# A gated feed-forward half in seven block products: the first pair's weights come through ACT's queue, and the tiles of a pair change places

## The chip, the core and the metric

The kernel runs on one core of a Trainium2 chip. Its engines are TensorE (PE in the profile, PEld for its weight loads), VectorE (DVE), ScalarE (ACT), GpSimd (POOL) and SyncE (SP). SP, ACT and POOL can each issue transfers between the chip's main memory and the core's on-chip memory; an engine's instructions, transfers among them, are taken in program order. The metric is the time of one execution on the device in microseconds (us).

## The reference

One decoder layer for 512 tokens of width 1024. Its first and last parts are feed-forward halves with a gate, and between them lie a gated linear recurrence with a short convolution, and attention into 256 memory rows. The change touches the two feed-forward halves alone:

```python
def swiglu(h, w_gate, w_up, w_down):
    return (jax.nn.silu(h @ w_gate) * (h @ w_up)) @ w_down
...
x = x + 0.5 * swiglu(rms_norm(x, ffn1_norm[l]), ffn1_gate[l], ffn1_up[l], ffn1_down[l])
...
x = x + 0.5 * swiglu(rms_norm(x, ffn2_norm[l]), ffn2_gate[l], ffn2_up[l], ffn2_down[l])
```

The hidden width is 2816, which is 22 tiles of 128.

## The kernel before, in words

Every float32 operand is split into a rounded high part and a low part that holds the rest (names that end in `h` and `l`, or `whi` and `wlo`), and a product is the sum of three: high by high, high weight by low input, low weight by high input. ACT makes the high part with a copy, DVE the low part with a subtraction that reads ACT's result. So no matmul of a weight tile starts before ACT's copy, and none with its `wlo` before DVE's subtraction.

The class `Half` holds a feed-forward half. Its hidden tiles 0 to 3 are computed plainly (`product`, `finish`). The other 18 go in 9 pairs, m = 4, 6, ..., 20 (`seven`). In a pair, gate and up weights and the input are cut into blocks, and seven block products take the place of eight: p1, p5, r6, p2, r7, p4, p3. Each is 24 matmuls with 256 columns. They need five weight tiles of 512 KB in all: b11, b22 and b21 are blocks as they lie in memory. t1 is a sum of two blocks: a plain transfer brings the first, and a second transfer, issued by POOL, adds the other to it as it lands. t3 is made in the same way, both transfers by POOL. p1 multiplies b11 by input `a11`, p5 multiplies t1 by `q1`, r6 multiplies t1 + b22 (DVE adds) by `n2`, p2 multiplies b21 by `a12`, r7 multiplies t3 by `d3`, p4 takes t1 + b22 + b21 by `a22`, and p3 takes b22 by `q4`.

`load` (line 293) issues the transfers of a pair. `unit` (line 312) splits a weight tile: the copy on ACT is line 316, the subtraction on DVE line 317. Matmuls of all seven products are line 338, the sum t1 + b22 is an addition from line 324.

Ahead of the first pair, `inputs_steps` (line 246) combines the normed input into the blocks that the products take. For that it uses six raw tiles: `xa0`, `qn0`, `xa1`, `qn1`, and the combinations `c0`, `c1`. They have the same tag as the weight tiles, in a ring of six (tag `raw`, line 257 and line 297), so the five weight tiles of pair 4 can only be loaded as these are given back. `quad` (line 236) splits an input block, ACT at line 242 and DVE at line 243. Blocks `a11`, `q1`, `n2` are split early; the splits of the other four are the list `later` (lines 285 to 289). `a12` and `a22` read `tx`, which is not in this ring; `d3` and `q4` read `c0` and `c1`, which are.

All this is done beside `down_pairs` (line 433): while PE multiplies the first four hidden tiles by the down weights in four steps (d = 0, 2, 4, 6; names `psd`, lines 119 to 121), three of the waiting steps are issued after each d. After d = 6 stands p1 of pair 4.

The text of the program is not the order in which an engine gets its instructions: a scheduler lays them out when the program is built, each engine's list is then fixed, and between engines only the waits order them. The places that matter below are those lists.

Of the kernel before, what the change touches and what calls it, by code (L numbers as in the profile page):

```python
# [38 lines left out]
def decoder_layer(ctx: ExitStack, tc: tile.TileContext, xT, memT, vecs, masks, ident_d,  # L39
                  w1, w1d, w_in, w_i, w_out, w_q, w_k, w_v, w_o, w2, w2d, gfin, out):  # L40
    nc = tc.nc
# [44 lines left out]
    def weights(src, shape):  # L86

        raw, hi, lo, load, split = weight_steps(src, shape)
        load(0, shape[0])
        split(0, shape[0])  # L90
        return hi, lo

    def weight_steps(src, shape):
        n = n_unit[0]
        n_unit[0] += 1
        raw = wpool.tile([P, 1024], F32, tag="raw", name=f"raw{n}")
        hi, lo = (wpool.tile([P, 1024], F32R, tag=t, name=f"{t}{n}") for t in ("whi", "wlo"))
        a, b = shape
        w = a * b

        def load(k0, k1, queue=nc.sync):
            c = slice(k0 * b, k1 * b)
            if len(src.shape) == 3:
                queue.dma_start(raw[:, c].rearrange("p (a b) -> p a b", a=src.shape[1]), src)
            else:
                queue.dma_start(raw[:, c], src[:, c])

        def split(k0, k1):
            c = slice(k0 * b, k1 * b)
            nc.scalar.activation(hi[:, c], raw[:, c], AF.Copy)  # L110
            nc.vector.tensor_tensor(lo[:, c], raw[:, c], r32(hi[:, c]), ALU.subtract)  # L111

        v = lambda t: t[:, :w].rearrange("p (a b) -> p a b", b=b)
        return raw, v(hi), v(lo), load, split
# [80 lines left out]
    CLASSIC = 4  # L195
    PARTS = ((0, 4), (4, 10), (10, 16), (16, FT))

    class Half:
# [47 lines left out]
        def inputs_steps(self):  # L246

            name, hp = self.name, self.hp
            self.q, later = {}, []
            sub = lambda o, a, b: nc.vector.tensor_tensor(o, a, b, ALU.subtract)  # L250

            def scaled(t, k):
                nc.vector.scalar_tensor_tensor(t, x[k], vec[:, self.gcol + k:self.gcol + k + 1], self.bc,
                                               op0=ALU.mult, op1=ALU.mult)


            raw = lambda key: hp.tile([P, 2, S], F32, tag="raw", name=f"{key}_{name}", bufs=6)
            self.tx = [hp.tile([P, 2, S], F32, tag=t, name=f"x{t}_{name}", bufs=4) for t in ("ah", "al")]
            tmps = [(raw(f"xa{n}"), raw(f"qn{n}")) for n in range(2)]
            self.tc = [raw(f"c{n}") for n in range(2)]  # L260
            steps = []
            for n in range(2):
                xb, comb = self.tx[n], self.tc[n]
                xa, qn = tmps[n]
                q1, n2 = qn[:, :, :256], qn[:, :, 256:]

                def one(n=n, xa=xa):
                    for i in range(2):
                        scaled(xa[:, i], 2 * n + i)
                    self.quad("a11", n, xa[:, :, :256])  # L270

                def two(n=n, xb=xb, xa=xa, q1=q1, n2=n2):
                    for i in range(2):
                        scaled(xb[:, i], 4 + 2 * n + i)
                    sub(q1, xa[:, :, 256:], xb[:, :, 256:])
                    sub(n2, q1, xa[:, :, :256])
                    self.quad("q1", n, q1)

                def three(n=n, xb=xb, comb=comb, xa=xa, n2=n2):
                    sub(comb[:, :, :256], xa[:, :, :256], xa[:, :, 256:])  # L280
                    nc.vector.tensor_tensor(comb[:, :, 256:], xb[:, :, :256], n2, ALU.add)
                    self.quad("n2", n, n2)

                steps += [one, two, three]
            for key in ("a12", "d3", "a22", "q4"):
                for n in range(2):
                    t = (self.tx if key[0] == "a" else self.tc)[n]
                    h = t[:, :, :256] if key in ("a12", "d3") else t[:, :, 256:]
                    later.append(lambda key=key, n=n, h=h: self.quad(key, n, h))
            return steps, later  # L290


        def load(self, m):


            def tile(key):
                return self.hp.tile([P, 2, 512], F32, tag="raw", name=f"{key}_{self.name}{m}", bufs=6)

            def src(j, h):
                return self.wgu[m:m + 2, j, :, h * 512:(h + 1) * 512].rearrange("m p c -> p m c")  # L300

            b11, t1, b22, b21, t3 = (tile(k) for k in ("b11", "t1", "b22", "b21", "t3"))
            nc.sync.dma_start(b11, src(0, 0))
            nc.sync.dma_start(t1, src(0, 0))
            nc.gpsimd.dma_start(t1, src(1, 0), accum_op=ALU.add)
            nc.sync.dma_start(b22, src(1, 1))
            nc.sync.dma_start(b21, src(0, 1))
            nc.gpsimd.dma_start(t3, src(1, 0))
            nc.gpsimd.dma_start(t3, src(1, 1), accum_op=ALU.add)
            return dict(b11=b11, t1=t1, b22=b22, b21=b21, t3=t3)  # L310

        def unit(self, raw):
# [250 lines left out]
    with tc.tile_pool(name="mix", bufs=8, reuse_waits="tile") as mp:  # L563
# [56 lines left out]
        for k2 in range(KT // 2):  # L620
            wh, wl = weights(w_i[k2], (2, 512))
            for kk in range(2):
                k = 2 * k2 + kk
# [512 lines left out]
```

## Time and profile before

| | |
|---|---|
| median of 3 runs | 1113.97 us (1113.47 to 1115.74) |
| the profiled execution, its own time | 1115.02 us |
| span of the profiled execution | 1113.2 us |
| PE busy | 1094.7 us |
| DVE busy | 731.2 us |
| ACT busy | 485.9 us |
| POOL busy | 74.6 us |
| mean granted clock of PE | 0.995 |

The span is the time from the first to the last instruction. A row of the timeline gives start, duration, engine, source line, operation, the tile written and the tiles read, and in brackets how long the engine stood idle before it and what ended that. PE's matmuls overlap: a matmul of 256 columns is shown with 0.28 us, yet the next one starts 0.12 us after it, so the distance between starts counts. "Landing" is the time from the issue of a transfer to its completion as the waiting engine sees it.

### The profile page before, as it was taken

What the parts mean: (1) busy time and instruction counts of PE and PEld (TensorE: products, weight loads), DVE (VectorE), ACT (ScalarE), POOL (GpSimd) and SP (SyncE); (2) the same over time, 40 slices, a digit from 0 to 9 for tenths busy, and PEclk for the clock granted to TensorE, in tenths of its full rate; (3) what the DMA queues carried; (4) which work ended last, traced back from release to release, by engine and by line L of the source; (5) the groups of instructions that cost most, each with busy time, mean ns of one, the idle gap of its engine ahead of it and who ended that gap; (6) DMA issues with size and microseconds to landing.
All of it is one profiled execution on the core that took longest, in us unless ns stands there. A gap on an engine that the chain in (4) does not pass through costs nothing. (4 is left out here: it accounts for less than half of the span.)

```text
span 1113.2 us, 15967 instructions
## 1 busy us (share of the span) xinstructions
PE 1094.7 (98%) x6528; PEld 979.4 (88%) x6528; DVE 731.2 (66%) x980; ACT 485.9 (44%) x667; POOL 74.6 (7%) x75
## 2 busy tenths in 40 slices
PE   9989999999999999999999999999989999999997
PEld 7869998998998888888889888888889989989995
DVE  6786755764768566885686556554987747755744
ACT  6435533542545344323364345342545524533553
POOL 0001100110100000000100000000011101100102
PEclk9999999999999999999999999999999999999999
DMA  6467764673523332222244324232287835764521
GB/s 210 127 177 172 195 143 125 164 194 116 160 45 110 97 100 80 81 76 85 67 120 138 122 77 133 74 96 78 84 230 190 186 109 137 203 146 135 114 76 76
DMA packets 68745, 140.53 MB, mean 126 GB/s; under 512 B 4944, under 2 KB 20560, under 8 KB 68672
## 3 DMA queue, kind: packets, MB, share of 16 engines
q1 hardware_dynamic: 54112, 108.02, 30.7%
q0 software_dynamic: 12544, 28.84, 13.2%
q10 hardware_dynamic: 2016, 2.66, 0.7%
q8 instruction: 51, 0.84, 0.3%
q14 instruction: 22, 0.18, 0.1%
HBM read 137.40 MB, written 2.10 MB: 125 GB/s over the span
## 5 line engine op out<-in xcount | busy, mean ns | idle before, releaser
L110 ACT ACTIVATE whi<-raw 128x1024 fp32r<-128x1024 f32 (+4 forms) x143 | 138.0, 970 | 329.5 <-issue 67.4
L111 DVE TENSOR_TENSOR wlo<-raw,whi 128x1024 fp32r<-128x1024 f32 (+4 forms) x143 | 158.6, 1112 | 83.7 <-ACT whi L110 83.1
L316 ACT ACTIVATE whi<-b_f 128x1024 fp32r<-128x1024 f32 x72 | 76.3, 1060 | 104.5 <-issue 34.3
L317 DVE TENSOR_TENSOR wlo<-b_f,whi 128x1024 fp32r<-128x1024 f32 x72 | 88.2, 1225 | 42.3 <-ACT whi L316 40.9
L120 PE MATMUL psd_f<-al_f,whi 128*128 128x512 f32 x280 | 109.1, 390 | 0.0
L121 PE MATMUL psd_f<-ah_f,wlo 128*128 128x512 f32 x280 | 109.1, 390 | 0.0
L119 PE MATMUL psd_f<-ah_f,whi 128*128 128x512 f32 x280 | 108.5, 390 | 0.0
L317 DVE TENSOR_TENSOR wlo<-t_f,whi 128x1024 fp32r<-128x1024 f32 x54 | 66.1, 1224 | 42.6 <-ACT whi L316 42.6
L192 DVE SCALAR_TENSOR_TENSOR xall<-psd_f,xall 128x512 f32<-128x512 f32 x52 | 35.4, 691 | 71.4 <-PE psd_f L121 71.4
L316 ACT ACTIVATE whi<-t_f 128x1024 fp32r<-128x1024 f32 x54 | 57.0, 1056 | 56.6 <-issue 21.3
L121 PEld LDWEIGHTS psd_f<-ah_f,wlo 128*128 128x128 f32 x280 | 52.6, 188 | 10.9
L119 PEld LDWEIGHTS psd_f<-ah_f,whi 128*128 128x128 f32 x280 | 52.6, 188 | 10.8
L120 PEld LDWEIGHTS psd_f<-al_f,whi 128*128 128x128 f32 x280 | 52.6, 188 | 10.7
L338 PE MATMUL psD_f<-q1h_f,whi 128*128 128x256 f32 x144 | 41.2, 286 | 8.3 <-ACT whi L316 8.3
L338 PE MATMUL psA_f<-a11h_f,wlo 128*128 128x256 f32 x144 | 42.2, 293 | 0.0
L338 PE MATMUL psA_f<-a11h_f,whi 128*128 128x256 f32 x144 | 42.1, 292 | 0.0
L338 PE MATMUL psA_f<-a11l_f,whi 128*128 128x256 f32 x144 | 42.1, 292 | 0.0
L338 PE MATMUL psD_f<-q1l_f,whi 128*128 128x256 f32 x144 | 41.0, 284 | 0.0
L338 PE MATMUL psA_f<-a22h_f,whi 128*128 128x256 f32 x144 | 40.9, 284 | 0.0
L338 PE MATMUL psD_f<-q4h_f,wlo 128*128 128x256 f32 x144 | 40.8, 284 | 0.0
L338 PE MATMUL psA_f<-n2h_f,wlo 128*128 128x256 f32 x144 | 40.8, 284 | 0.0
L338 PE MATMUL psA_f<-a22h_f,wlo 128*128 128x256 f32 x144 | 40.8, 284 | 0.0
(778 smaller groups left out, 3209.7 us busy)
## 6 DMA issues: line engine op xcount, KB each, us to landing
b_f<-in_w SPq DMA_DIRECT2D x54, 512.0 KB, 4.0
t_f<-in_w POOLq DMA_DIRECT2D x54, 512.0 KB, 5.7
raw<-in_w_in SPq DMA_DIRECT2D x24, 512.0 KB, 3.5
t_f<-in_w SPq DMA_DIRECT2D x18, 512.0 KB, 5.3
raw<-in_w1d SPq DMA_DIRECT2D x20, 384.0 KB, 3.1
raw<-in_w SPq DMA_DIRECT2D x13, 512.0 KB, 3.5
raw<-in_w2d SPq DMA_DIRECT2D x16, 384.0 KB, 3.1
raw<-in_w2d SPq DMA_DIRECT2D x10, 512.0 KB, 3.4
```

Of the source, the lines that this page charges most:

```text
L110: nc.scalar.activation(hi[:, c], raw[:, c], AF.Copy)
L111: nc.vector.tensor_tensor(lo[:, c], raw[:, c], r32(hi[:, c]), ALU.subtract)
L119: nc.tensor.matmul(out, lhsT=wh, rhs=xh, start=first, stop=False)
L120: nc.tensor.matmul(out, lhsT=wh, rhs=xl, start=False, stop=False)
L121: nc.tensor.matmul(out, lhsT=wl, rhs=xh, start=False, stop=last)
L192: nc.vector.scalar_tensor_tensor(x[k], ps, scale, x[k], op0=ALU.mult, op1=ALU.add)
L316: nc.scalar.activation(hi, raw, AF.Copy)
L317: nc.vector.tensor_tensor(lo, raw, r32(hi), ALU.subtract)
L338: nc.tensor.matmul(o, lhsT=a[:, i, w], rhs=b, start=first and i == 0 and k == 0 and n == 0, stop=k == 3 and n == 2, skip_group_check=True)
```

## The change

Three things are changed, all in `Half`:

- the splits of the input blocks in `later` come in another order: `d3` and `q4` of c0, then of c1, then `a12` and `a22`;
- in every pair, t3 takes its tile from the ring ahead of b22 and b21, and its two transfers are written ahead of those of b22 and b21;
- for pair 4 alone (`CLASSIC` is 4), the transfers of b11, t1 and b22 are issued by ACT. b21 stays with SP, and the other pairs stay with SP as they were.

```diff
-            for key in ("a12", "d3", "a22", "q4"):
-                for n in range(2):
+            for keys in (("d3", "q4"), ("a12", "a22")):
+                for n, key in ((n, key) for n in range(2) for key in keys):
                     t = (self.tx if key[0] == "a" else self.tc)[n]
                     h = t[:, :, :256] if key in ("a12", "d3") else t[:, :, 256:]
                     later.append(lambda key=key, n=n, h=h: self.quad(key, n, h))
...
-            b11, t1, b22, b21, t3 = (tile(k) for k in ("b11", "t1", "b22", "b21", "t3"))
-            nc.sync.dma_start(b11, src(0, 0))
-            nc.sync.dma_start(t1, src(0, 0))
+            b11, t1, t3, b22, b21 = (tile(k) for k in ("b11", "t1", "t3", "b22", "b21"))
+
+            queue = nc.scalar if m == CLASSIC else nc.sync
+            queue.dma_start(b11, src(0, 0))
+            queue.dma_start(t1, src(0, 0))
             nc.gpsimd.dma_start(t1, src(1, 0), accum_op=ALU.add)
-            nc.sync.dma_start(b22, src(1, 1))
-            nc.sync.dma_start(b21, src(0, 1))
             nc.gpsimd.dma_start(t3, src(1, 0))
             nc.gpsimd.dma_start(t3, src(1, 1), accum_op=ALU.add)
+            queue.dma_start(b22, src(1, 1))
+            nc.sync.dma_start(b21, src(0, 1))
```

Lines behind the change have numbers higher by two (before's lines 316 and 338 are 318 and 340). The lists of the engines move as follows; the first half's pair 4 is shown, and the second half's moves alike. In the names, `f1` is the first half, the digit behind it the pair or the block half, and the last number a running one.

ACT's list ahead of pair 4, before. The five rows with a `c` or `x` tile behind the arrow are input splits, the last two the copies of b11 and t1; no transfer stands here, since SP issues all four plain ones.

```order
L242 ACTIVATE n2h_f11_624<-qn1_f1_407 128x512
L242 ACTIVATE d3h_f11_668<-c1_f1_409 128x512
L242 ACTIVATE a22h_f10_672<-xah_f1_402 128x512
L242 ACTIVATE a22h_f11_704<-xal_f1_403 128x512
L242 ACTIVATE q4h_f10_708<-c0_f1_408 128x512
L242 ACTIVATE q4h_f11_712<-c1_f1_409 128x512
L316 ACTIVATE whi12_729<-b11_f14_716 128x1024
L316 ACTIVATE whi13_760<-t1_f14_717 128x1024
```

The same place of the change:

```order
L242 ACTIVATE n2h_f11_624<-qn1_f1_407 128x512
L305 DMA b11_f14_716<-in_w1 128x2x512
L242 ACTIVATE d3h_f11_664<-c1_f1_409 128x512
L242 ACTIVATE q4h_f11_668<-c1_f1_409 128x512
L242 ACTIVATE a12h_f10_672<-xah_f1_402 128x512
L242 ACTIVATE a22h_f10_704<-xah_f1_402 128x512
L242 ACTIVATE a12h_f11_708<-xal_f1_403 128x512
L242 ACTIVATE a22h_f11_712<-xal_f1_403 128x512
L306 DMA t1_f14_717<-in_w1 128x2x512
L310 DMA b22_f14_719<-in_w1 128x2x512
L318 ACTIVATE whi12_729<-b11_f14_716 128x1024
L318 ACTIVATE whi13_760<-t1_f14_717 128x1024
```

The transfer of b11 stands behind the last split of `n2`; that of t1 stands behind six further splits, of which the first two read `c1`. On POOL, t3's plain transfer now stands ahead of the adding transfer of t1; on SP, b21 of pair 4 stands alone ahead of pair 6.

PE's list at the start of p1, before: `a11` with b11's halves (whi12, wlo12) is p1, `q1` with t1's (whi13, wlo13) is p5.

```order
L338 MATMUL psA_f14_728<-a11h_f10_430,whi12_729 128x256
L338 MATMUL psA_f14_728<-a11l_f10_431,whi12_729 128x256
L338 MATMUL psD_f14_759<-q1h_f10_510,whi13_760 128x256
L338 MATMUL psD_f14_759<-q1l_f10_511,whi13_760 128x256
L338 MATMUL psA_f14_728<-a11h_f10_430,wlo12_730 128x256
```

And of the change:

```order
L340 MATMUL psA_f14_728<-a11h_f10_430,whi12_729 128x256
L340 MATMUL psA_f14_728<-a11l_f10_431,whi12_729 128x256
L340 MATMUL psA_f14_728<-a11h_f10_430,wlo12_730 128x256
L340 MATMUL psA_f14_728<-a11h_f10_430,whi12_729 128x256
L340 MATMUL psA_f14_728<-a11l_f10_431,whi12_729 128x256
```

The two `q1` matmuls that stood third and fourth are now behind all 24 of `a11`. Instead, two matmuls of p2 (b21, `a12`) stand after the first two of r6 (t1 + b22, `n2`):

```order
L340 MATMUL psA_f14_728<-n2l_f10_571,whi14_789 128x256
L340 MATMUL psB_f14_819<-a12h_f10_672,whi15_820 128x256
L340 MATMUL psB_f14_819<-a12l_f10_673,whi15_820 128x256
L340 MATMUL psA_f14_728<-n2h_f10_570,wlo14_790 128x256
```

DVE's list keeps its length up to b11's `wlo`: the same number of splits and additions stands ahead of it, the splits in the new order.

At the program's start, ACT's list has a transfer behind splits and squares, the same in both programs:

```order
L125 ACTIVATE x_f14h_202<-xall_102,vec_97 128x512
L125 ACTIVATE x_f15h_215<-xall_102,vec_97 128x512
L125 ACTIVATE x_f16h_228<-xall_102,vec_97 128x512
L125 ACTIVATE x_f17h_241<-xall_102,vec_97 128x512
L136 ACTIVATE sq_f1_254<-xall_102 128x512
L136 ACTIVATE sq_f1_258<-xall_102 128x512
L502 DMA ident_99<-in_ident_d 128x128
```

Five activations stand between `x_f14h` and the transfer of `ident`; the change leaves this place as it is.

## The prediction

> **What bounds the kernel now.** I read the page's list of engines first, then the waits of PE, then the timeline of each engine around the two places that the waits name. The page:
>
> ```profile
> span 1113.2 us, 15967 instructions
> PE 1094.7 (98%) x6528; PEld 979.4 (88%) x6528; DVE 731.2 (66%) x980; ACT 485.9 (44%) x667; POOL 74.6 (7%) x75
> ```
>
> PE stands idle for 18.5 us in all. The waits of PE, the whole list (who waited, for whom, us in total, times, longest):
>
> ```profile
> PE psD_f L338 <- ACT whi L316: 8.3, 2, 5.0
> PE ps_f L119 <- ACT whi L110: 1.6, 2, 0.8
> PE warm L71 <- DVE mhalf L61: 1.1, 1, 1.1
> PE psw L119 <- ACT yh1h L811: 0.5, 1, 0.5
> ```
>
> Only the first row lies in the pairs of block products, twice: once in each half, in pair 4. The other 16 pairs have no wait on PE. So all that the change can gain lies at two places, and what it costs elsewhere must first use up slack. The first place, by PE's rows (MATMUL alone):
>
> ```profile
> 75.95 0.28 PE L338 MATMUL psA_f<-a11h_f,whi 128*128 128x256 f32 x1
> ...
> 76.07 0.28 PE L338 MATMUL psA_f<-a11l_f,whi 128*128 128x256 f32 x1
> 81.37 0.53 PE L338 MATMUL psD_f<-q1h_f,whi 128*128 128x256 f32 x1 [5.02 <-ACT whi L316]
> ...
> 82.77 0.41 PE L338 MATMUL psA_f<-a11h_f,whi 128*128 128x256 f32 x1
> 82.98 0.42 PE L338 MATMUL psA_f<-a11l_f,whi 128*128 128x256 f32 x1
> ...
> 94.24 0.28 PE L338 MATMUL psA_f<-d3h_f,whi 128*128 128x256 f32 x1
> ```
>
> After two matmuls of `a11` PE is held by the first of `q1`, which needs t1, and 22 matmuls of `a11` that need only b11 stand behind it. Then matmuls come 0.21 us apart, where 0.12 is usual (75.95 to 76.07). The stretches show the clock (us, PE busy, granted clock, DMA share, GB/s):
>
> ```profile
> 82.00:86.00 4.00, 4.00 (x25) 0.64 0.68 167
> 86.00:90.00 4.00, 4.00 (x36) 1.00 1.09 194
> 822.00:826.00 4.00, 4.00 (x24) 0.57 0.92 276
> ```
>
> About 16 matmuls run at half clock after each wait, which costs 16 x 0.09 = 1.45 us besides the wait. Who makes t1 late is read from SP, POOL, ACT and DVE, in this order:
>
> ```profile
> 66.71 0.46 SPq L304 DMA_DIRECT2D t_f<-in_w  x1
> 72.27 1.28 POOL L305 DMA_DIRECT2D t_f<-in_w  x1 [43.96 <-DMA t_f<-in_w]
> 80.27 1.06 ACT L316 ACTIVATE whi<-t_f 128x1024 fp32r<-128x1024 f32 x1 [7.18 <-DMA t_f<-in_w]
> 77.71 1.23 DVE L317 TENSOR_TENSOR wlo<-b_f,whi 128x1024 fp32r<-128x1024 f32 x1
> 81.35 1.23 DVE L317 TENSOR_TENSOR wlo<-t_f,whi 128x1024 fp32r<-128x1024 f32 x1 [2.42 <-ACT whi L316]
> 82.61 1.23 DVE L324 TENSOR_TENSOR t_f<-t_f,b_f 128x1024 f32<-128x1024 f32 x1
> 85.04 1.23 DVE L317 TENSOR_TENSOR wlo<-t_f,whi 128x1024 fp32r<-128x1024 f32 x1 [1.20 <-ACT whi L316]
> ```
>
> t1 is issued at 66.71, its adding transfer at 72.27, and ACT copies it at 80.27. I call this last time T: 13.56 us after the issue, two landings in a row. The second half has the same shape with a shorter adding:
>
> ```profile
> 808.72 0.46 SPq L304 DMA_DIRECT2D t_f<-in_w  x1
> 814.57 1.21 POOL L305 DMA_DIRECT2D t_f<-in_w  x1 [39.43 <-DMA t_f<-in_w]
> 820.40 1.06 ACT L316 ACTIVATE whi<-t_f 128x1024 fp32r<-128x1024 f32 x1 [5.45 <-DMA t_f<-in_w]
> 821.51 0.39 PE L338 MATMUL psD_f<-q1h_f,whi 128*128 128x256 f32 x1 [3.29 <-ACT whi L316]
> 834.37 0.28 PE L338 MATMUL psA_f<-d3h_f,whi 128*128 128x256 f32 x1
> ```
>
> In both halves r7's first matmul (`d3`) starts 13.97 us after T (94.24 - 80.27 and 834.37 - 820.40). From T on, the pair is one chain.
>
> **Part 1: PE's new order, a gain.** All of `a11` now stands ahead of `q1`. b11's `wlo` is the limit there: it ends at 77.71 + 1.23 = 78.94, because DVE has its splits and the sums of `psd` to do first, and as many stand ahead of it in the new list. So PE still idles from 76.35 to 78.94. Then 22 matmuls of `a11` take 22 x 0.12 = 2.64 us, to 81.6, ahead of `q1`. They leave the chain behind T.
>
> What that chain then is: `q1` may start at T + 1.1 (81.37 - 80.27), and go on when t1's `wlo` ends, at T + 2.31 (82.58); 22 matmuls bring T + 4.95. But the sum t1 + b22 takes its own way through DVE and ACT: its `wlo` ends at 85.04 + 1.23 = 86.27, which is T + 6.0. That is later, so it takes over as the bound: from T + 6.0, 22 matmuls of `n2` and 22 of `a12` are left, 44 x 0.12 = 5.3 us. The two `a12` that now stand third and fourth need b21's copy, which ACT makes right behind that of the sum, at about T + 5.85; they cost nothing more. `d3` then starts at T + 11.3. If the half clock falls into that stretch, up to 1.45 us come on top. I take 0.5, since most of such a phase would lie before T + 6.0, where PE waits anyway: T + 11.8. Gain against 13.97: 2.17 us a half, between 1.2 and 2.7.
>
> By the Trainium skill (TensorE: Matmul & The Clock Gate, section What's actually happening) the clock halves after an idle window of about 3.4 us; the new gaps, 2.6 us and then under 1, would be too short for it and the sum would be 1 us lower. This trace has half clock after a gap of 3.29 us too, so a window that is only mostly idle seems to do, and I keep the 0.5.
>
> **Part 2: t1 through ACT's queue, a loss.** On ACT the transfer of t1 stands behind six splits, and the second of them reads all of `c1`. When can ACT issue it? The row of `c1`'s last addition in each half, and ACT at the program's start:
>
> ```profile
> 69.30 0.69 DVE L281 TENSOR_TENSOR c_f<-xal_f,qn_f 128x512 f32<-128x512 f32 x1
> ...
> 811.17 0.69 DVE L281 TENSOR_TENSOR c_f<-xal_f,qn_f 128x512 f32<-128x512 f32 x1
> ```
>
> ```profile
> 13.97 0.71 ACT L125 ACTIVATE x_f14h<-xall,vec 128x512 fp32r<-128x512 f32 x1
> 14.29 0.34 ACTq L502 DMA_DIRECT2D ident<-in_ident_d  x1
> 14.59 0.70 ACT L125 ACTIVATE x_f15h<-xall,vec 128x512 fp32r<-128x512 f32 x1
> ```
>
> There the transfer of `ident` stands five activations behind `x_f14h`, yet it is issued 0.32 us after that one started, before the next had run. So ACT's queue hands out activations whose inputs are ready and comes to the transfer early. Splits behind `q4` of `c1` wait for nothing. So t1 goes out about 0.3 us after `c1` is complete: 69.99 + 0.3 = 70.3, and 811.86 + 0.3 = 812.2. That is 3.6 and 3.5 us later than SP issues it now; ring places are no help, since t1's own was free before 66.71.
>
> Landing of t1 (line 304) and of its adding (line 305), least, median, most:
>
> ```profile
> DMA to landing us min/median/max: 4.5/5.3/8.5
> ```
>
> ```profile
> DMA to landing us min/median/max: 5.5/5.7/7.9
> ```
>
> By the medians with 0.1 for two hand-overs, T is 11.1 us after the issue: 81.4 and 823.3. Against 80.27 and 820.40 that is 1.1 and 2.9 us later, though the first half's adding, 8.0 us in the trace, is granted its median. Bounds: 10.1 us by the least of both, and 13.6 us as in the first half now.
>
> **Part 3: the rest, nothing.** t3's plain transfer goes first on POOL and waits for nothing late; its adding stands behind t1's as before. b21 waits on SP for `q4` of `c0`, which DVE now does early, and is needed at T + 4.7. In the other pairs t3's tile comes free earlier, and b21's only after b11's split in p1; four products (p4, p3, p5, r6), 4 x 2.88 = 11.5 us, still lie ahead of its use and cover its landing, 5.8 us at most (line 307):
>
> ```profile
> DMA to landing us min/median/max: 3.4/4.5/5.8
> ```
>
> Without that cover a late b21 would hold PE in p2. Three issues on ACT cost no activation time: in the rows above `x_f15h` follows `x_f14h` after 0.62 us, less than the 0.71 that one is shown with.
>
> **The sum.** -2 x 2.17 + 1.1 + 2.9 = -0.3 us. The profiled execution took 1115.02 us, 1.05 over the median of 1113.97, so 1114.7 against that one, and 1113.6 against the median. Ends: both gains 2.7 with both T at 10.1 us give -3.3 (1110.7); gains 1.2 with 13.6 us give +6.6 (1120.6).
>
> **The rivals.**
>
> *Slower: ACT holds the transfer.* If ACT issues t1 only when its engine gets there, the place is that of the last split. In the trace the last two of five splits run from 71.00 to 72.14, 0.62 us the last:
>
> ```profile
> 71.00 1.14 ACT L242 ACTIVATE q4h_f<-c_f 128x512 fp32r<-128x512 f32 x2
> ```
>
> With one split more the last of them starts at about 72.1 and t1 goes out then, which is 1.8 us after 70.3, in both halves: +3.6 - 0.3 = +3.3, 1117.3 us. It decides when the issue is over 1.3 us later than I have it. The rows of `ident` speak against it. Chance 0.16.
>
> *Slower: a long adding.* t3's adding now follows t1's within about 1.2 us on POOL, and b22 and b21 are under way then too. If both take 7.9 us instead of 5.7, T moves by 2.2 twice: +4.1, 1118.1 us. For it speaks the first half's 8.0, against it the second's 5.8 with the same neighbours. Chance 0.09.
>
> *Faster: short landings and full clock.* t1 is alone at the head of ACT's ring instead of 0.5 us behind b11. With 10.1 us and T + 11.3 it is -3.3, 1110.7 us; over half of that must come true to be seen. Chance 0.13.
>
> *It does not do what it says.* The loads were to leave SP so as to come sooner; by the built order b11 and t1 both come later. That is part of the forecast and not a case of its own.
>
> The Trainium skill (DMA: Bandwidth & Descriptors, section Issuing engines are not separate DMA queues) says that issuing from several engines saves only the sequencer's issue time; by it part 2 could gain no landing time at all.
>
> **How the numbers follow.** A measurement of this kernel can tell about 0.2%, 2.2 us. Forecast: within that, 0.62, at 1113.6 us. Slower by more, 0.25; faster by more, 0.13. The range from 1110.9 to 1118.4 takes in the faster case nearly to its end and both slower ones; beyond it are combinations of bounds.
>
> **What would show it.** Right: PE's wait at `q1` is split into one of about 2.5 us for DVE's `wlo` of b11 and one for t1; ACT issues t1 near 70.3 and 812.2; T is near 81.4 and 823.3; `d3` starts 11.3 to 12.7 us after T; a short new wait stands at `n2` for DVE's `wlo`. Wrong: t1 issued before 69 or after 71.5, T outside 80.4 to 83.9 in the first half, a new wait in a later pair, or a `d3` that follows T by 13.5 us or more.

## The result, and the profile after

The changed kernel takes 1120.14 us (median of 6 runs, 1116.72 to 1124.99) beside 1114.84 us for the kernel before on the same chip (6 runs, 1113.47 to 1115.74). The ratio is 1.0052, with a 95% interval from 1.0029 to 1.0075: slower by 5.3 us, where 1113.6 and no change had been forecast. Its profiled execution took 1119.98 us. First its page, span and engines:

```profile
span 1118.2 us, 15957 instructions
PE 1097.7 (98%) x6528; PEld 980.5 (88%) x6528; DVE 731.2 (65%) x980; ACT 486.0 (43%) x667; POOL 74.7 (7%) x75
```

The span is 5.0 us longer, and PE is busy 3.0 us longer with as many matmuls: some of them ran slower. PE's waits (who, for whom, us in total, times, longest):

```profile
PE psA_f L340 <- DVE wlo L319: 5.3, 2, 2.6
PE psD_f L340 <- ACT whi L318: 3.5, 2, 2.3
PE ps_f L119 <- ACT whi L110: 1.8, 2, 1.3
PE psD_f L340 <- DVE wlo L319: 1.3, 2, 0.8
```

The wait for t1's copy has fallen from 8.3 to 3.5 us, and a wait of 2 x 2.6 us for DVE's `wlo` of b11 has come, as forecast. There is no new wait in a later pair. So the loss lies in pair 4 of the two halves again, and there in T, the time at which ACT copies t1, and in what follows it. The chain of the first half, by the timelines of ACT, POOL and PE:

```profile
69.68 0.38 ACTq L306 DMA_DIRECT2D t_f<-in_w  x1
74.96 1.25 POOL L307 DMA_DIRECT2D t_f<-in_w  x1 [4.57 <-DMA t_f<-in_w]
82.89 1.06 ACT L318 ACTIVATE whi<-t_f 128x1024 fp32r<-128x1024 f32 x1 [9.55 <-PE psA_f L340]
95.24 0.28 PE L340 MATMUL psA_f<-d3h_f,whi 128*128 128x256 f32 x1
```

And of the second:

```profile
812.98 0.37 ACTq L306 DMA_DIRECT2D t_f<-in_w  x1
817.54 1.20 POOL L307 DMA_DIRECT2D t_f<-in_w  x1 [3.79 <-DMA t_f<-in_w]
826.06 1.06 ACT L318 ACTIVATE whi<-t_f 128x1024 fp32r<-128x1024 f32 x1 [9.43 <-DMA t_f<-in_w]
839.38 0.28 PE L340 MATMUL psA_f<-d3h_f,whi 128*128 128x256 f32 x1
```

t1 is issued as forecast, at 69.68. The last of the splits that stand ahead of this transfer in ACT's list starts only 2.1 us later:

```profile
71.77 0.62 ACT L242 ACTIVATE a22h_f<-xal_f 128x512 fp32r<-128x512 f32 x1
```

But t1's adding takes 7.93 and 8.52 us (74.96 to 82.89, 817.54 to 826.06) where 5.7 had been put. And `d3` follows T by 12.35 and 13.32 us where 11.8 had been put. The stretches from T to `d3` show why (us, busy time of PE, PEld, DVE, ACT and POOL, granted clock, DMA share, GB/s):

```profile
82.89:95.24 12.35, 10.49 (x72) 10.28 (x73) 8.40 (x7) 6.14 (x7) 1.95 (x2) 0.85 0.71 158
826.06:839.38 13.32, 11.71 (x72) 11.41 (x73) 8.40 (x7) 6.14 (x7) 1.95 (x2) 0.74 0.62 144
```

The clock is 0.85 and 0.74 there. Since everything ahead of pair 4 is shifted a little from one execution to the next, I count from PE's first `a11` of the pair (75.95 and 817.82 before, 75.60 and 818.89 after) to the first `d3`. That is 18.29 and 16.55 us before, 19.64 and 20.49 after: 5.3 us more in sum, which is the whole loss.

What is it that meets the adding? The page's rows of the DMA queues, for the second half's adding alone (packets, MB, share of the 16 engines' time), before the change and after; q0 is POOL's queue, q1 SP's, q10 ACT's:

```profile
q0 software_dynamic: 306, 0.66, 70.0%
q1 hardware_dynamic: 272, 0.51, 24.0%
```

```profile
q0 software_dynamic: 376, 0.73, 46.3%
q1 hardware_dynamic: 570, 1.10, 39.4%
q10 hardware_dynamic: 233, 0.44, 13.5%
```

In both the engines are busy nearly all the time (94% and 99%). What changed in this half is whose bytes they carry: 1.54 MB of SP's and ACT's queues in place of 0.51 MB. In the first half the adding was long before the change already, 8.00 us beside 0.97 MB on POOL's queue and 0.70 MB on SP's; after it, it takes 7.93 us beside 0.68 MB on POOL's and 1.33 MB on SP's and ACT's.

Back in the second half, at least 0.58 MB of SP's 1.10 MB is no load of pair 4 at all, since b21, its only one there, has 0.52 MB. SP's rows for the first tile of pair 6, before and after, second half:

```profile
819.70 0.37 SPq L303 DMA_DIRECT2D b_f<-in_w  x1
```

```profile
817.16 0.37 SPq L305 DMA_DIRECT2D b_f<-in_w  x1
```

Counted from the first `a11` it is issued 1.88 us behind it before, and 1.73 us ahead of it after. What set it free is DVE's split `q4l` of c1; before and after:

```profile
818.98 0.69 DVE L243 TENSOR_TENSOR q4l_f<-c_f,q4h_f 128x512 fp32r<-128x512 f32 x1
```

```profile
816.45 0.68 DVE L243 TENSOR_TENSOR q4l_f<-c_f,q4h_f 128x512 fp32r<-128x512 f32 x1
```

The ring has six places and pair 4 takes five. The sixth, c1's, goes to pair 6's b11. The new order splits `q4` of c1 as the fourth of eight in place of the last, c1's place comes free 3.6 us earlier, and SP, which now has only b21 ahead, issues pair 6's b11 at once: into t1's adding. The prediction didn't see that. Whether it is the cause, the experiments had to show.

### The profile page after: what moved, and what is told of

Read it like the earlier page. It is cut to its first block, busy times and chain, and to the rows that moved or that the text cites. A ratio compares the mean times of both kernels' runs of the same rounds, so it can differ in the third digit from the quotient of the medians.

```text
span 1118.2 us, 15957 instructions
## 1 busy us (share of the span) xinstructions
PE 1097.7 (98%) x6528; PEld 980.5 (88%) x6528; DVE 731.2 (65%) x980; ACT 486.0 (43%) x667; POOL 74.7 (7%) x75
## 5 line engine op out<-in xcount | busy, mean ns | idle before, releaser
L319 DVE TENSOR_TENSOR wlo<-t_f,whi 128x1024 fp32r<-128x1024 f32 x54 | 66.1, 1224 | 51.0 <-ACT whi L318 51.0
L340 PE MATMUL psD_f<-q1h_f,wlo 128*128 128x256 f32 x144 | 42.6, 296 | 1.3 <-DVE wlo L319 1.3
L340 PE MATMUL psA_f<-n2l_f,whi 128*128 128x256 f32 x144 | 41.0, 285 | 0.0
L340 PE MATMUL psA_f<-n2h_f,whi 128*128 128x256 f32 x144 | 41.0, 285 | 0.0
L340 PE MATMUL psB_f<-a12h_f,whi 128*128 128x256 f32 x144 | 41.0, 285 | 0.0
```

The source lines that it names most:

```text
L319: nc.vector.tensor_tensor(lo, raw, r32(hi), ALU.subtract)
L340: nc.tensor.matmul(o, lhsT=a[:, i, w], rhs=b, start=first and i == 0 and k == 0 and n == 0, stop=k == 3 and n == 2, skip_group_check=True)
```

## The experiments

Each run has been compared with the kernel before on its own chip, where that one takes 1114.88 us (e1 to e4), 1115.36 (e5 to e8), 1116.19 (e9 to e12) or 1115.41 (e13 to e15). So it is the ratios that can be set side by side, not the medians. The last two columns are from one profiled execution of each kernel, by the rows of the first `a11`, of ACT's copy of t1 (T) and of the first `d3`. The table has all runs; they are told in turn below.

| kernel | us, median | ratio to before (95%) | T behind the first a11, by half | first a11 to d3, by half |
|---|---|---|---|---|
| before | 1114.84 | | 4.32, 2.58 | 18.29, 16.55 |
| after | 1120.14 | 1.0052 (1.0029 to 1.0075) | 7.29, 7.17 | 19.64, 20.49 |
| e1 t3 behind t1's adding | 1118.49 | 1.0036 (1.0022 to 1.0050) | 7.53, 6.46 | 19.87, 19.97 |
| e2 without t3's adding | 1120.52 | 1.0048 (1.0035 to 1.0061) | 7.69, 7.06 | 20.04, 20.20 |
| e3 without ACT's queue | 1120.40 | 1.0046 (1.0034 to 1.0058) | 6.78, 5.52 | 20.93, 20.11 |
| e4 new order alone | 1117.59 | 1.0029 (1.0018 to 1.0040) | 6.89, 6.58 | 18.53, 18.90 |
| e5 b11 and t1 of pair 6 held | 1114.50 | 0.9997 (0.9986 to 1.0007) | 6.32, 5.44 | 17.83, 16.96 |
| e6 ACT's queue alone | 1128.83 | 1.0122 (1.0108 to 1.0135) | 11.16, 10.81 | 24.17, 23.94 |
| e7 filled gaps | 1119.66 | 1.0046 (1.0030 to 1.0062) | 8.08, 9.81 | 20.42, 23.37 |
| e8 early t1, early wlo of b11 | 1106.11 | 0.9914 (0.9901 to 0.9926) | -5.42, -5.42 | 13.10, 13.11 |
| e9 new order alone, pair 6 held | 1114.04 | 0.9979 (0.9970 to 0.9988) | 5.21, 5.31 | 16.97, 17.06 |
| e10 b21 loaded twice | 1115.83 | 0.9996 (0.9987 to 1.0005) | 4.11, 4.19 | 18.08, 19.32 |
| e11 early t1 alone | 1106.87 | 0.9925 (0.9912 to 0.9937) | -3.98, -3.97 | 13.82, 13.80 |
| e12 early t1, both wlo early | 1106.12 | 0.9911 (0.9897 to 0.9924) | -5.42, -5.42 | 13.09, 13.10 |
| e13 t1 of pair 6 held | 1121.45 | 1.0055 (1.0042 to 1.0068) | 7.42, 9.47 | 20.54, 21.75 |
| e14 b11 of pair 6 held | 1112.69 | 0.9981 (0.9970 to 0.9992) | 6.04, 4.24 | 17.55, 15.75 |
| e15 before, early t1 alone | 1109.45 | 0.9948 (0.9934 to 0.9962) | -4.58, -4.57 | 13.82, 14.76 |

### Is it t3's adding? (e1, e2)

The rival of the prediction with the right size, a long adding, named t3's adding as the cause: it is issued 0.8 and 1.4 us behind t1's. So this was theory A, and two runs took it away. In e1:

```diff
-            nc.gpsimd.dma_start(t1, src(1, 0), accum_op=ALU.add)
-            nc.gpsimd.dma_start(t3, src(1, 0))
+            added = nc.gpsimd.dma_start(t1, src(1, 0), accum_op=ALU.add)
+            with tc.issue_after(added.ins):
+                nc.gpsimd.dma_start(t3, src(1, 0))
```

> The kernel after, with t3's plain transfer queued behind t1's adding on POOL, so that t3's own adding can't be issued before that plain transfer has landed (about 5 us later). Theory A (t1's adding takes 7.9 and 8.5 us after the change because t3's adding is issued 0.8 and 1.4 us behind it): it takes 5.7 again, ACT's copy of t1 comes 2.2 and 2.8 us earlier (80.7 and 823.3 in place of 82.9 and 826.1), and the time falls by 4 to 5 us, to 1115.5. Rival B (it is lengthened by b22, b21 and the next b11, which are under way as well): the adding stays at 8 us, the time at 1120.

And in e2:

```diff
-            nc.gpsimd.dma_start(t3, src(1, 1), accum_op=ALU.add)
+            if m > CLASSIC:
+                nc.gpsimd.dma_start(t3, src(1, 1), accum_op=ALU.add)
```

> The kernel after, with t3's adding left out in pair 4 of both halves: r7 there works on the first of t3's two blocks alone. Nothing else is moved. Theory A (t3's adding lengthens t1's): t1's adding takes 5.7 us, the copy of t1 comes at 80.7 and 823.3, time 1115.5. Rival B (the plain transfers lengthen it): the adding stays at 7.9 and 8.5, time 1120. If the adding is short here and long with t3's plain transfer behind it, a plain transfer on POOL's queue is enough.

Theory A falls. POOL and ACT of e2 in the second half, with no adding of t3 in pair 4:

```profile
816.99 1.20 POOL L307 DMA_DIRECT2D t_f<-in_w  x1 [3.39 <-DMA t_f<-in_w]
...
825.78 1.06 ACT L319 ACTIVATE whi<-t_f 128x1024 fp32r<-128x1024 f32 x1 [9.33 <-PE psA_f L341]
```

t1's adding takes 8.79 us, and 1.86 MB of SP's and ACT's queues pass meanwhile. In e1, with t3's adding over 11 us later, it takes 8.4 and 8.3 us.

### The parts of the change alone (e3, e4, e6)

e3 sets `queue = nc.sync` for every pair; e4 is the kernel before with the new loop over `later` alone; e6 is the kernel before with b11, t1 and b22 of pair 4 on `nc.scalar` alone.

> The kernel after, with b11, t1 and b22 of pair 4 issued by SP again; ring places and the order of the splits as after. PE's list goes back to 2 of a11, 2 of q1, 22 of a11. t1 is then issued near 66.4 and its adding near 72. Theory A: t3's adding waits for its plain transfer (issued near 69.6, 5 us) and comes 3 us behind t1's, so that t1's adding takes 5.7 to 7; T at 78 to 79.5 and about 820.5, d3 at T + 13.97 as before: 1112 to 1115. Rival (the order of splits and ring places cost the time, not ACT's queue): 1120.

> The kernel before with the new order of the splits alone: all loads on SP, ring places as before. PE's list has all of a11 ahead of q1, as after, and POOL has t3's plain transfer ahead of t1's adding. My prediction's part 1 says that this order is worth 2.2 us a half if t1 comes no later than before: T near 78 to 80.3 and 820.4, d3 at T + 11.8, 1110. Rival (more and shorter gaps of PE cost as much in half clock as the order saves; after the change d3 came at T + 12.35 and T + 13.3): 1113 to 1115.

> The kernel before with ACT's queue alone: b11, t1 and b22 of pair 4 are issued by ACT; ring places and the order of the splits as before. t1 is issued near 70 as after the change and its adding near 75. Theory B: with the old order of the splits c1's ring place comes free late, pair 6's b11 is issued near 77 or later and not at 73.9, so t1's adding meets less and takes 6 to 7 us, T near 81.5 and 823; 1116 to 1118. Rival (ACT's queue itself makes the adding long): 8 us or more, T at 83 and 826, 1120 or more.

Without ACT's queue the loss stays (e3), and the new order alone makes half of it (e4), outside both of its forecasts. So the loss doesn't need ACT's queue. e3 does not price that queue by itself, though: PE's list is there the one of before, with two of `q1` behind two of `a11`, and `d3` follows T by 14.15 and 14.59 us, while T, counted from the first `a11`, is 0.5 and 1.65 us earlier than after the change. Both runs issue t1 early, at 66.1, and its adding at 71.9 and 72.6, and yet T comes 6.78 and 6.89 us behind the first `a11` in the first half, hardly earlier than the 7.29 of the change. In both, pair 6's b11 goes out at 73.6.

e6 came out worse than any forecast for it. POOL in its first half says why:

```profile
76.15 0.78 POOL L309 DMA_DIRECT2D t_f<-in_w  x1 [47.99 <-DVE q4l_f L243]
76.93 1.29 POOL L306 DMA_DIRECT2D t_f<-in_w  x1
```

t3's plain transfer stands ahead of t1's adding in POOL's list. With the old ring places and the old order it waits for the split `q4` of c0, whose place it takes, and t1's adding waits behind it, goes out at 76.93 and takes 10.0 us beside t3's plain transfer and pair 6's loads (77.68 and 78.82). So ACT's queue alone costs 1.2%, more than twice what the whole change does: the new order and ring places take most of that away.

### Is it the loads of pair 6? (e5, e13, e14, e9, e10)

In e5 ACT writes two columns of pair 6's b11 tile from pair 4's sum before the load may overwrite them. The load of t1 is queued behind it:

```diff
+            if m == CLASSIC + 2:
+                with tc.high_priority():
+                    nc.scalar.activation(b11[:, :, :1], self.t1_before[:, :, :1], AF.Copy)
+            self.t1_before = t1
-            queue.dma_start(b11, src(0, 0))
-            queue.dma_start(t1, src(0, 0))
+            first = queue.dma_start(b11, src(0, 0))
+            with tc.issue_after(first.ins):
+                queue.dma_start(t1, src(0, 0))
```

> The kernel after, with the first two loads of pair 6 (b11 and t1, by SP) held until pair 4's sum t1 + b22 is made: ACT writes two columns of pair 6's b11 tile from that sum, and the load overwrites them. After the change these two loads go out at 73.87 and 78.61, inside t1's adding (74.96 to 82.89); before it at 77.83 and 78.96. Theory B (t1's adding shares the DMA engines with whatever the hardware queues carry: 1.10 + 0.23 MB and 1.10 + 0.44 MB during the adding after, 0.70 and 0.51 MB before): the hardware queues carry 0.5 to 0.6 MB less, 2 us at 255 to 269 GB/s, t1's adding takes 6 to 6.5 us, T comes near 81 and 823.8, time 1115.5 to 1116.5. Rival (the adding is slow by itself through POOL's queue; runs without t3's adding and with it delayed left T where it was): T stays at 82.9 and 826.1, time 1120.

1114.50, 0.9997 of the kernel before: the whole loss is gone. t1's adding takes 6.1 and 6.2 us (75.96 to 82.07, 816.25 to 822.43). In the second half the clock stays full and `d3` follows T by 11.52 us:

```profile
822.43:833.95 11.52, 9.81 (x77) 9.18 (x76) 8.31 (x7) 6.14 (x8) 1.99 (x2) 1.00 0.59 151
```

Which of the two loads is it? In e13 the columns are written into pair 6's t1 tile, and b11 goes out early as after the change. In e14 they are written into b11's, and t1 goes first when its own place comes free.

> The kernel after, with pair 6's t1 alone held until pair 4's sum is made; pair 6's b11 goes out as after the change, near 73.9 and 817.2. If the early b11 is what lengthens t1's adding: T stays near 82.9 and 826, time 1118.5 to 1120. If it is t1's load at 78.6 and 821.9: the time falls to 1114.5 to 1116, as with both held (1114.5). If only the sum of bytes counts, about half of the 5 us comes back: 1117.

> The kernel after, with pair 6's b11 alone held until pair 4's sum is made; pair 6's t1 goes out first, when its ring place comes free, near 78.6 and 821.9. If the early b11 lengthens t1's adding, T comes to 81 to 82 and 823 to 824.3 as with both held, time 1114.5 to 1116. If it is t1's load: 1118.5 to 1120. If only the sum of bytes counts: 1117.

It is b11, which goes out first. With it early (74.06 and 818.01) and t1 held, 1121.45; with it held and t1 at 77.94 and 818.98, 1112.69: 8.8 us apart, although the same loads are made. Both came out beyond their ranges, e13 slower and e14 faster, and why e14 lies below e5, where t1 is held too, isn't shown; their intervals just overlap. In e13's second half, moreover, it is the landing of t1 itself that is long, 8.0 us (813.82 to 821.83), and the adding takes 7.4. Here are the queues from t1's issue to T in the second half, after the change (812.98 to 826.06) and in e14 (810.05 to 820.21):

```profile
q0 software_dynamic: 503, 1.23, 39.6%
q10 hardware_dynamic: 678, 1.29, 30.2%
q1 hardware_dynamic: 570, 1.10, 25.6%
```

```profile
q0 software_dynamic: 477, 1.17, 48.6%
q10 hardware_dynamic: 686, 1.31, 35.0%
q1 hardware_dynamic: 272, 0.52, 13.3%
```

POOL's and ACT's queues moved nearly the same. SP's moved 1.10 MB against 0.52, b21 alone. Its share of the engines was 25.6% of 13.08 us, 3.35 us, against 13.3% of 10.16 us, 1.35 us. So 2.0 of the 2.9 us by which T follows the issue of t1 more closely in e14 are the engines' time for SP's further bytes. In the first half the same sum fits less well: 26.2% of 13.21 us against 11.6% of 11.96 is 2.1 us, and T follows the issue only 1.25 us more closely. The Trainium skill (DMA: Bandwidth & Descriptors, section Issuing engines are not separate DMA queues) says that transfers run on the same 16 engines and interleave, whichever engine has issued them. These rows agree: a load from SP's queue lengthened a chain that went through ACT's and POOL's.

e9 holds pair 6's b11 and t1 in the kernel with the new order alone, e4:

> The kernel before with the new order of the splits (as in the run of the order alone) and with pair 6's first two loads held until pair 4's sum is made. This takes the collision out of the order. If theory B is the whole of it, the order is then worth what part 1 of the prediction gave it: t1's adding is issued near 72.6 and 814.7 and takes 6 to 7.5 us, T at 78.7 to 80.2 and 820.8 to 822.2, d3 at T + 11.5; the time from PE's first a11 to d3 is 15 to 16.3 us a half (before 18.29 and 16.55), time 1110 to 1112.5. Rival (the gain of the order is lost in half clock whatever the transfers do): 1114 to 1115.

It is faster than e4 by 1.0029 - 0.9979, 0.5% or 5.6 us, and than the kernel before by 0.2%. That lies between the two theories: the order is worth about 2.3 us once pair 6's loads don't collide with it, half of what part 1 had given it. Part 1's own term is there in full: `d3` follows T by 11.76 and 11.75 us, 2.2 less than before. But T is late, 5.21 and 5.31 us behind the first `a11` (before 4.32 and 2.58), since the adding still takes 8.0 us.

Here t3's plain transfer stands 0.8 us ahead of it on POOL, POOL's queue carries 1.08 MB during the adding, and SP's only 0.35 and 0.38. So pair 6's loads are not the only thing that goes with a long adding. In the halves whose t1 isn't loaded early, five addings took 5.8 to 6.2 us (before's second, both of e5 and of e14), with at most 0.70 MB on POOL's queue and 0.52 on SP's meanwhile; all others took 7.1 us or more, with at least 0.94 MB on POOL's or 0.70 on SP's. That goes together and shows no cause by itself, for a longer adding also lets more pass.

The reverse, more traffic in the kernel before, was e10:

```diff
-            nc.sync.dma_start(b21, src(0, 1))
+            for _ in range(2 if m == CLASSIC else 1):
+                nc.sync.dma_start(b21, src(0, 1))
```

> The kernel before with b21 of pair 4 loaded twice by SP, the same data into the same tile, the second time behind the first one's landing. Nothing else is moved: SP then issues pair 6's loads as before or somewhat later. Theory B: 0.52 MB more in the hardware queues while t1's adding runs; at 250 to 270 GB/s it takes 2 us longer in each half, T at 82 and 822.5, time 1118 to 1119. Rival (a transfer of the hardware queues costs the adding nothing; what counts is POOL's own queue): 1114 to 1115.

This missed. The second load went out at 74.6. In the second half the adding took 7.45 us beside 1.10 MB of SP's (before 5.83 beside 0.51), about what theory B gives; in the first it took 7.54 beside 1.03 MB (before 8.00 beside 0.70), and the time is 0.9996 of before. So half a megabyte more beside the adding doesn't always cost the 2 us that I had worked out from bytes. What makes b11 of pair 6 dear and the second b21 cheap isn't settled by these runs.

### The half clock (e7)

18 matmuls that nobody reads stand behind the first two of `a11`, and 9 behind the last. They write the bank of `q1`, which is therefore taken at the start of p1:

```diff
+                            if m == CLASSIC and quad == "a11":
+                                count = 18 if (i, k, n) == (0, 0, 1) else 9 if (i, k, n) == (1, 3, 2) else 0
+                                for _ in range(count):
+                                    nc.tensor.matmul(st["D"][:, 0], lhsT=wh[:, 0, :P], rhs=self.q["a11"][0][0][:, 0],
+                                                     start=True, stop=True, skip_group_check=True)
...
+                room("D")
                 multiply("A", st["raw"]["b11"], "a11", True)
...
-                room("D")
                 multiply("D", st["raw"]["t1"], "q1", True)
```

> The kernel after, with matmuls that nobody reads in two of PE's gaps of pair 4: 18 behind the first two of a11 (where PE waits for DVE's wlo of b11) and 9 behind the last of a11 (where it waits for ACT's copy of t1), into the bank that q1's first matmul then starts afresh. T isn't touched. Theory C (about 2 us of the loss are half clock: d3 follows T by 12.35 and 13.3 us and not by 11.3): the granted clock stays at 1.00 between 80 and 92, d3 follows T by 11.3 to 11.8, time 1117.5 to 1118.5, with less spread from run to run than the 8 us of after. Rival (the clock falls whatever stands in the gaps, or d3 is bound by the sum t1 + b22 alone): 1120, same spread.

The stretches of the first half:

```profile
80.00:84.00 4.00, 2.23 (x19) 2.03 (x17) 0.00 (x0) 0.69 (x1) 0.00 (x0) 1.00 1.11 228
84.00:88.00 4.00, 2.83 (x15) 2.62 (x16) 2.45 (x2) 1.93 (x4) 0.77 (x1) 0.80 0.37 107
88.00:92.00 4.00, 4.00 (x29) 4.00 (x28) 3.96 (x4) 1.98 (x2) 0.42 (x1) 0.77 0.78 118
```

The fillers kept the clock full from 80 to 84, where PE would have waited anyway. They did not keep it behind T, where it counts: 0.80 and 0.77, and `d3` at T + 12.34. In the second half T came so late that PE waited 3.92 us behind the fillers. The runs lie 9 us apart, no less than after the change. As a cure the fillers fail.

They leave the size of the half clock to be read from the rows alone, in the halves in which PE has all of `a11` ahead of `q1` and T comes behind the first `a11`: `d3` follows T by 11.5 to 11.6 us where the clock is 1.00 (e14 in both halves, e5 in the second, e4 in the first), by 12.3 to 12.4 us in six halves at 0.77 to 0.86 (the first of after, e1, e2 and e7, the second of e4 and e13), and by 13.0 to 13.6 us in seven at 0.71 to 0.75. So half clock behind T costs 0.8 us, or 1.5 to 2 us, in these.

It need not cost anything: in three halves the mean clock is 0.87 or 0.90 and `d3` comes 11.5 to 11.8 us behind T (e5's first, both of e9). In e5's the half clock ends by T + 3 (0.50 and 0.51 from 82.07 to 85.00, 1.00 behind it), well ahead of T + 6.0, up to which the sum t1 + b22 holds PE anyway:

```profile
82.07:93.58 11.51, 11.26 (x82) 10.75 (x80) 8.31 (x7) 6.24 (x8) 1.98 (x2) 0.87 0.58 149
```

After the change, first half, matmuls stand 0.21 us apart from 86.56 to 89.74, which is T + 3.7 to T + 6.9.

### Loading t1 early (e8, e11, e12, e15)

If t1 is late, why wait for the other splits? The tiles for b11 and t1 can be taken behind the third step of the splits. e8 does so on ACT's queue and puts DVE's `wlo` of b11 ahead of the later splits:

```diff
+                def early(n=n, three=three):
+                    three()
+                    if n == 0:
+                        self.early = self.first(CLASSIC, nc.scalar)
-                steps += [one, two, three]
+                steps += [one, two, early]
...
+                if m == CLASSIC and key == "A" and first:
+                    with tc.high_priority():
+                        wh, wl = self.unit(raw)
```

`first` takes the tiles of b11 and t1 and issues their loads and t1's adding, t1 first in pair 4. e11 leaves the `wlo` of b11 where it was, e12 puts that of t1 ahead as well, and e15 is the kernel before with `early` alone.

> The kernel after, with t1 and b11 of pair 4 loaded by ACT's queue as soon as the third step of the splits has been traced (t1 first), some 12 us ahead of now, and DVE's wlo of b11 ahead of the later splits. If the lateness of t1 and of b11's wlo is the whole cost at this place, PE finds everything ready: its waits at psA and psD go, and with them the half clock that follows. From before: 8.3 us of waits and about 2 x 1.45 us of half clock go, 1104 us. Rival (the two transfers only push the loads of the down projection's weights back, so that PE waits there): 1109 to 1115.

> The early load of t1 and b11 alone, with DVE's wlo of b11 left where the order of the splits puts it (near 77.4). It parts the two causes that the early load with the early wlo took away together. PE's list is then again 2 of a11, 2 of q1, 22 of a11. PE still waits for that wlo, 2.3 us in each half, and half clock may follow: the time lies 2 x 2.3 to 2 x 3.5 us over that run's 1106.1, at 1110.5 to 1113. Rival (t1 was all that mattered): 1106 to 1107.

> The early load with DVE's wlo of t1 put ahead of the later splits as well as that of b11. In the run with the wlo of b11 alone PE was left with two waits of 0.8 us for the wlo of t1 and two of 0.2 us. If nothing comes in their place: 1104 to 1105, the best of all. Rival (the splits that are pushed back by 1.2 us hold PE later, at a22 or n2): 1106.

> The kernel before with the early load alone: t1 and b11 of pair 4 through ACT's queue right behind the third step of the splits, old order of the splits, old ring places, no change of DVE's order. If the lateness of t1 was all that the two places cost, none of the change's three parts is needed for the gain: T near 72, PE waits about 2 us a half for DVE's wlo of b11, 1106 to 1108. Rival (the old order of the splits keeps b22 or b21 back, so that the sum t1 + b22 comes late): 1109 to 1112.

All four beat both kernels; t1 is issued at 49.19 in e8, earlier than I had thought. e8 gains 9.6 us by its ratio, where 11 had been added up. PE's waits in e8:

```profile
PE psD_f L355 <- DVE wlo L330: 1.6, 2, 0.8
PE ps_f L119 <- ACT whi L110: 1.5, 2, 0.9
PE warm L71 <- DVE mhalf L61: 1.1, 1, 1.1
PE psw L119 <- ACT yh1h L828: 0.5, 1, 0.5
PE psB_f L355 <- ACT whi L329: 0.5, 2, 0.2
```

t1 is copied 5.4 us before PE gets to the pair, the clock stays at 1.00, and the way from `a11` to `d3` is 13.1 us in each half. The early load alone (e11) gives 0.9925. The `wlo` of b11 adds 0.1%, which the intervals don't part; I had expected 0.4% or more, since I put half clock behind a wait of 2 us, and there was none. The `wlo` of t1 (e12) adds nothing: short waits for ACT come in its place. On the old order and ring places (e15) the early load is worth 0.5%, as its rival had it; there t3's plain transfer goes out at 75.05 and not at 69.41 as in e11, but no wait of PE names t3. So the new order and ring places may be worth 0.2% once t1 is out of the way, at the edge of what the intervals part.

## Why the prediction was wrong, point by point

**What bounds the kernel: right.** Two places, and T and the stretch behind it in each. From first `a11` to `d3` the sum of the halves goes from 34.84 us (before) to 40.13 (after), 48.11 (e6) and 26.21 (e8), that is by +5.3, +13.3 and -8.6 us; the ratios make it +5.8, +13.6 and -9.6 us. Only in e7 and e10 do the two differ by more than 1.6 us.

**Part 1, PE's new order: right in its steps, too small in its half clock.** The wait for b11's `wlo` is 2.64 us as worked out, `a11` leaves the chain, and at full clock `d3` follows T by 11.5 us, between the 11.3 and the 11.8 given. But I granted half clock 0.5 us, "since most of such a phase would lie before T + 6.0, where PE waits anyway", and it cost 0.85 and 1.8: there are now three gaps for it to follow in each half, not one, and it ran on past T + 6.0. That is 2.1 us of the miss (12.35 + 13.32 - 2 x 11.8). The short wait forecast at `n2` did not come, since PE got there late: at T + 6.2 in the first half, when the `wlo` of the sum had been ready since T + 5.9.

**Part 2, when t1 goes out: right.** 69.68 and 812.98 are 5.92 and 5.91 us ahead of the first `a11`, forecast were 5.65 and 5.62. The issue ahead of splits that have yet to run, read from `ident`, holds. The rival "ACT holds the transfer" is thereby out.

**Part 2, the landing: the step that failed.** "By the medians with 0.1 for two hand-overs, T is 11.1 us after the issue." It is 13.21 and 13.08. Counted from the first `a11`, T is 1.84 and 1.69 us later than forecast (7.29 and 7.17 in place of 5.45 and 5.48), 3.5 us of the miss. With part 1's 2.1 us and the forecast's own -0.3 this is the 5.3 us measured. t1's own landing, 5.28 and 4.56 us, was no longer than the 5.3 granted; the term that was too small is the adding, 7.93 and 8.52 us for 5.7. The first half's adding of 8.0 us stood in the trace, and I granted it its median; a median of a transfer's landing holds for the traffic that it was taken in.

**Part 3, "the rest, nothing": the cause of that.** I followed `q4` of c0, which gives b21 its place, and not `q4` of c1 in the same list, which gives pair 6's b11 its place. That load left 3.6 us earlier on a queue that I had declared free of the change. Where it alone is held (e14), the adding takes 6.13 and 5.86 us, and the changed kernel 0.9981 of before: 2.1 us less, where 0.3 less had been forecast and 5.3 more came.

**The signs: too loose.** None of the signs of being wrong that were listed came. The issue, the first half's T (82.89) and `d3` (at most T + 13.32) lie inside the bounds given, and no later pair waits. For the second half's T, 826.06 where 823.3 had been put, no bound was listed.

**The rival "a long adding"** gave 1118.1 us for 7.9 us in both halves, near what came, with a wrong cause: without t3's adding (e2) nothing gets better.

**The Trainium skill's rule on the clock.** By the Trainium skill (TensorE: Matmul & The Clock Gate, section What's actually happening) the clock halves after an idle window of about 3.4 us, and the window runs free of the program. The same wait for `wlo`, 2.64 us in both halves of e14, is followed by half clock in the first and not in the second, as the next rows show. That agrees with a window that runs free, and not with a rule by which PE has to rest for 3.4 us:

```profile
78.00:80.00 2.00, 2.00 (x9) 2.00 (x10) 0.00 (x0) 0.00 (x0) 0.00 (x0) 0.50 1.14 193
820.00:822.00 2.00, 2.00 (x18) 1.93 (x17) 0.70 (x1) 1.12 (x2) 0.00 (x0) 1.00 1.15 206
```

**What stays open.** Why the second b21 of e10 cost so little. And why the landing of t1 itself varies: after the change and in e7, whose transfers are the same, it took 4.56 and 7.96 us in the second half. These are e7's rows:

```profile
813.11 0.37 ACTq L306 DMA_DIRECT2D t_f<-in_w  x1
...
821.07 1.20 POOL L307 DMA_DIRECT2D t_f<-in_w  x1 [7.19 <-DMA t_f<-in_w]
```

The runs of the changed kernel lie 8 us apart, those of the kernel before on the same chip 2 us. On other chips the kernel before spreads by 4 to 6 us as well. That this landing is the reason is likely, but it was not tried. Pair 6's b11 went out inside both of the long landings, at 817.30 in e7 and at 818.01 in e13; whether that lengthened them was not tried either.

## What to carry to other kernels

When a change moves the last reader of a buffer, list everything that gets that buffer next, on every queue, and look at what it will run beside: here one load that left 3.6 us early, and that ACT copied only 19 us after its issue (73.87 to 92.68), made the difference between 0.9981 and 1.0052. Price a transfer by the traffic at its new place, not by its median elsewhere. And where the head of a chain is late, start it earlier before shortening what follows: loading t1 some 20 us sooner (49.19 in e8, 69.68 after the change) was worth 0.75% on the new order and 0.5% on the old one (e15), when all the reordering behind it was worth 0.2% at best.

## What was not expected of the hardware

An adding transfer takes more of the engines' time for a megabyte than a plain one. In e5's first adding 0.70 MB of q0 had 73.4% of 6.11 us, 6.4 us per MB, and 0.36 MB of q1 15.4%, 2.6 us per MB:

```profile
q0 software_dynamic: 357, 0.70, 73.4%
q1 hardware_dynamic: 193, 0.36, 15.4%
```

It is the adding and not POOL's queue. In e2's first half t1's adding is all that this queue carries while it runs (75.84 to 82.95), and 0.52 MB take 46.5% of 7.11 us, 6.4 us per MB again: as much as all 16 engines in 3.3 us. After the change the plain transfer of t3 is all that it carries from 812.98 to 817.54, and 0.50 MB take 27.0% of 4.56 us, 2.5 us per MB, like a plain load of SP's. e2's row:

```profile
q0 software_dynamic: 272, 0.52, 46.5%
```
